# The last two product units of a stage taken chunk by chunk, with up to four output units of a feed-forward pass held back

## The chip, the cores and the metric

The kernel runs on one core of one Trainium2 chip. The metric is the device time of one execution in microseconds (us); the figure for a kernel is the median of its runs. TensorE (PE) multiplies matrices, VectorE (DVE), ScalarE (ACT) and GpSimd (POOL) work on tiles in on-chip memory, SyncE (SP) issues the DMA transfers that bring weights in.

## The reference

Two blocks work on x, 256 tokens of 1024 numbers. The first has two layers of `x = x + mixer(x); x = x + peer_ffn(x)`, where `peer_ffn` gathers from 16384 experts (128 units of 128). The second has two layers of

```python
x = x + 0.5 * m[2] * swiglu(modulate(x, norm_g[l, 0], m[0], m[1]), ffn1_wi[l], ffn1_wo[l])
if ctx_in:
    ctx = ctx + 0.5 * mc[2] * swiglu(modulate(ctx, norm_g[l, 0], mc[0], mc[1]), ffn1_wi[l], ffn1_wo[l])
h = modulate(x, norm_g[l, 1], m[3], m[4])
...
x = x + m[5] * y
...
x = x + 0.5 * m[8] * swiglu(modulate(x, norm_g[l, 2], m[6], m[7]), ffn2_wi[l], ffn2_wo[l])
```

with `swiglu(h, wi, wo)` = `(silu(a) * u) @ wo`, `a, u = split(h @ wi)`, 2816 wide (22 times 128). `modulate` is an RMS norm with a gain, a scale and a shift. `mc` and `ctx` are a second, 256 tokens long sequence, the context, which is used in the first of the two layers alone. At the end comes `rmsnorm(x, final_g)`.

## The kernel before, in words

**Data.** x is held transposed: 128 partitions, 8 chunks, 256 tokens. A weight unit is 128x1024 fp32. It is loaded (`raw`, L85), ACT rounds it to fp32r (`whi`, L93), and DVE or POOL makes the remainder (`wlo`, L97). The activations are split in the same way (`xnh` and `xnl`, `ch` and `cl`, `hh` and `hl`). Each product is three matmuls, hi by hi, hi by lo, lo by hi (`mm3`, L170 to L172), so that a unit takes 24 matmuls.

**Stages.** mix0, peer0, mix1, peer1, then ffn1_0, mixb0, ffn2_0 (layer 0 of the second block) and ffn1_1, mixb1, ffn2_1 (layer 1), then the final norm. All but the final norm end alike: `up` (L200) adds the last units into four PSUM banks with two chunks of 128x256 each (`acc`), and `residual` (L205) adds the eight chunks to x. The next stage begins with the norm of x: eight squares on ACT (`sq`, L225, two buffers), eight matmuls against ones (`nps`, L226), square root on ACT (`rstd`, L216), reciprocal on DVE (L217). Most stages take the norm's factor out of the product: `scaled` (L234) makes `xnh` and `xnl` from x alone, and the factor is applied to the products, so that the stage's first matmuls need x and not `rstd`. mixb0, mixb1 and the final norm need `rstd` first (`norm`, L260: `ny`, then `xnh` and `xnl`).

**A feed-forward pass** (`ffn`, L985). 22 rounds: two units `wi` (`ff`), SiLU and gate (`t`, `hh`, `hl`), one unit `wo` into `acc`. The output unit of a round is multiplied one round later (lag 1). A pass for x has a room (`Room`, L971) with its own stream of `wi` units of three buffers (`F_RAW`, `F_BUFS`), of which the first six `wlo` are made by POOL (`LEAD_I`); the `wo` units go through the main stream, also three buffers. The pass over the context `xc` works inside mixb0, in a room without a stream, and its matmuls stand among those of mixb0's projections.

**Order.** The order of each engine's instructions is found when the program is built, by a scheduler that takes the program's order as the priority and plays the engines through in time. A buffer that is used again adds a wait for its last reader. On-chip memory is handed out by rooms, so that a larger room takes addresses that another tile could have had.

Of the kernel before, what the change touches and what calls it, by code (L numbers as in the profile page):

```python
# [9 lines left out]
F32 = mybir.dt.float32  # L10
F32R = mybir.dt.float32r
I32 = mybir.dt.int32
U32 = mybir.dt.uint32
AF = mybir.ActivationFunctionType
OP = mybir.AluOpType
# [3 lines left out]
T = 256  # L19
NDC = 8  # L20
# [19 lines left out]
N_REC = 6  # L40
PAT_F = "v"
X_DMA = 4
F_RAW = 3
F_BUFS = 3
PAT_R = "v"
PAT_G = "v"
NF = 22

CAND = [(0, 1, 16, 0), (1, 2, 8, 16), (2, 4, 5, 24), (4, 8, 3, 34), (8, 16, 1, 46)]
NCAND = 54  # L50
# [50 lines left out]
class Net:  # L101
# [100 lines left out]
            s = slice(dc * 128, (dc + 1) * 128)  # L202
            self.mm3(acc[dc // 2][:, dc % 2], (w[0][:, s], w[1][:, s]), h, first and dc % 2 == 0, last)

    def residual(self, x, acc, gate=None):  # L205
        nc = self.nc
        for dc in range(NDC):
            if gate is None:
                nc.vector.tensor_tensor(out=x[:, dc], in0=acc[dc // 2][:, dc % 2], in1=x[:, dc], op=OP.add)
            else:  # L210
                nc.vector.scalar_tensor_tensor(out=x[:, dc], in0=acc[dc // 2][:, dc % 2], scalar=gate[:, dc:dc + 1],
                                               in1=x[:, dc], op0=OP.mult, op1=OP.add)
# [92 lines left out]
def hgrn_gmlp(n: Net):  # L305
    nc, d = n.nc, n.d
    n.rotation = ["mm", "ac", "mm", "ac", "mm", "ac", "ac"]
    n.stream.pattern = PAT_0
    with ExitStack() as st:
        p = st.enter_context(n.tc.tile_pool(name="m0", bufs=1, reuse_waits="tile"))  # L310
        w2 = st.enter_context(n.tc.tile_pool(name="m0w", bufs=2, reuse_waits="tile"))
        xn, rn = n.scaled(n.x, n.v("l0_norm_mix"), None, None, p)
# [152 lines left out]
        for h in range(4):  # L465
# [6 lines left out]
            nc.scalar.activation(out=q, in_=ps, func=AF.Square)  # L472
            squares.append([(q, 0, 128)])
        rs = n.head_rstd(p, sel, squares, 128)
        for h in range(4):
            y = w2.tile([128, T], F32, tag="y", name="y")
            nc.vector.scalar_tensor_tensor(out=y, in0=oo[:, h], scalar=n.v("hgrn_g")[:, h:h + 1], in1=rs[h],
                                           op0=OP.mult, op1=OP.mult)
            nc.vector.tensor_tensor(out=y, in0=y, in1=og[:, h], op=OP.mult)
            yh = w2.tile([128, T], F32R, tag="yh", name="yh")  # L480
            yl = w2.tile([128, T], F32R, tag="yl", name="yl")
            n.split(y, yh, yl)
            n.up(acc, n.unit(d["w0_out"][h]), (yh, yl), False, h == 3)
        n.residual(n.x, acc)

def peer(n: Net, layer, mod, mod_upto):
# [4 lines left out]
    with ExitStack() as st:  # L493
# [4 lines left out]
        xn = []  # L498
# [118 lines left out]
        with ExitStack() as sg:  # L617
            gp = sg.enter_context(n.tc.tile_pool(name="gg", bufs=1, reuse_waits="tile"))
            gg = gp.tile([128, 128 - NS, T], F32, name="gg")
            onehot = n.tc.tile_pool(name="oneh", bufs=OH, reuse_waits="tile")  # L620
            o2 = onehot.__enter__()
            for t0 in range(0, T, 4):
                a = o2.tile([128, 4, 128], F32, tag="oa", name="oa")
                b = o2.tile([128, 4, 128], F32, tag="ob", name="ob")
                g = n.bank("gps").rearrange("p (t e) -> p t e", t=4)


                by_act = t0 // 4 % N_ACT == 1
                for t in range(4):
                    at = lambda s: it[:, s, t0 + t:t0 + t + 1]  # L630
                    nc.vector.tensor_scalar(out=a[:, t], in0=n.iota, scalar1=at(0), scalar2=None, op0=OP.is_equal)
                    if by_act:
                        nc.scalar.activation(out=b[:, t], in_=n.iota, func=AF.Abs, scale=-1.0, bias=at(1))
                        nc.scalar.activation(out=b[:, t], in_=b[:, t], func=AF.Relu, scale=-2.0, bias=at(2))
                    else:
                        nc.vector.tensor_scalar(out=b[:, t], in0=n.iota, scalar1=at(1), scalar2=at(2),
                                                op0=OP.is_equal, op1=OP.mult)
                for t in range(4):
                    nc.tensor.matmul(g[:, t], a[:, t], b[:, t], start=t == 0, stop=True, skip_group_check=True)  # L639
                ge = g.rearrange("p t e -> p e t")  # L640
                nc.vector.tensor_tensor(out=ca[:, :, t0:t0 + 4], in0=ca[:, :, t0:t0 + 4], in1=ge[:, 0:NS], op=OP.mult)
                nc.scalar.copy(out=gg[:, :, t0:t0 + 4], in_=ge[:, NS:128])  # L642
            n.stream.pattern = PAT_G
            onehot.__exit__(None, None, None)
            g2 = sg.enter_context(n.tc.tile_pool(name="gg2", bufs=2, reuse_waits="tile"))

            def coef(i):
                return ca[:, i] if i < NS else gg[:, i - NS]

            acc = []  # L650

            def up(i):
                if not acc:
                    acc.extend(n.accs())
                w = n.unit(d[pre + "up"][i])
                c = coef(i)
                ch = g2.tile([128, T], F32R, tag="ch", name="ch")
                cl = g2.tile([128, T], F32R, tag="cl", name="cl")
                n.split(c, ch, cl)
                n.up(acc, w, (ch, cl), i == 0, i == 127)  # L660

            done = 0
            for i in range(NS, 128, 2):
                def sink(b):
                    nc.scalar.activation(out=b, in_=b, func=AF.Gelu_apprx_tanh)
                    c = gg[:, i - NS:i - NS + 2]
                    nc.vector.tensor_tensor(out=c, in0=c, in1=b, op=OP.mult)  # L667
                if i == NS + 2 * N_PARK:
                    while mod.next < mod_upto:
                        mod.step(n.main.raw_p)  # L670
                    mod.bank = None
                down_pair(i, sink, "ac" if i < NS + 2 * N_PARK else None)
                while i >= NS + 2 * N_PARK and done < i + 2 - N_LAG:
                    up(done)
                    done += 1
            while done < 128:
                up(done)
                done += 1
            n.residual(n.x, acc)

# [288 lines left out]
class Room:  # L971


    def __init__(self, n, st, tag, own=False):
        pool = lambda name, bufs: st.enter_context(n.tc.tile_pool(name=name + tag, bufs=bufs, reuse_waits="tile"))
        self.p = pool("f", 1)
        self.w2 = pool("g", 2 if own else 3)
        self.xn = pool("fx", 1) if own else None
        self.more = None if own else Stream(n, st, "f", F_RAW, F_BUFS)
        if not own:  # L980
            self.more.pattern = n.main.pattern = PAT_F
            self.more.lead, n.main.lead = LEAD_I, n.main.count + LEAD_O


def ffn(n: Net, x, mod, cond, which, wi, wo, gvec, tag, room=None):  # L985

    nc = n.nc
    with ExitStack() as st:
        room = room or Room(n, st, tag)
        p, w2 = room.p, room.w2  # L990
        gain = mod.gain(which + 1, cond, gvec)
        gate = mod.gate(which + 2, cond, 0.5)
        xn, r = n.scaled(x, gain, mod.m[:, which, cond], room.xn, p)
        acc = n.accs()
        late = None
        for f in range(NF + 1):
            if f < NF:
                t = []
                c = w2.tile([128, 2], F32, tag="c", name="c")
                for u in range(2):  # L1000
                    b = n.bank("ff")
                    w = (room.more or n).unit(wi[f, u])
                    n.proj_t(b[:, 0:T + 2], w, xn)
                    t.append(w2.tile([128, T], F32, tag=f"t{u}", name=f"t{u}"))
                    nc.vector.tensor_copy(out=c[:, u:u + 1], in_=b[:, T:T + 1])
                    nc.vector.tensor_tensor(out=t[u], in0=b[:, 0:T], in1=r, op=OP.mult)
                s = t[0]
                nc.scalar.activation(out=s, in_=s, func=AF.Silu, bias=c[:, 0:1])
                hh = w2.tile([128, T], F32R, tag="hh", name="hh")
                hl = w2.tile([128, T], F32R, tag="hl", name="hl")  # L1010
                if f < NF - 1:
                    nc.vector.scalar_tensor_tensor(out=s, in0=t[1], scalar=c[:, 1:2], in1=s, op0=OP.add, op1=OP.mult)
                    n.split(s, hh, hl)
                else:
                    for o in (hh, s):
                        nc.vector.scalar_tensor_tensor(out=o, in0=t[1], scalar=c[:, 1:2], in1=s, op0=OP.add, op1=OP.mult)
                    nc.vector.tensor_tensor(out=hl, in0=s, in1=hh.bitcast(F32), op=OP.subtract)  # L1017
                now = (f, n.main.unit(wo[f]), (hh, hl))
            if late is not None:
                n.up(acc, late[1], late[2], late[0] == 0, late[0] == NF - 1)  # L1020
            late = now
        n.residual(x, acc, gate)


def gla_decay(n, p, w2, zg, wa2, tag, smask):
# [613 lines left out]
```

## Time and profile before

| | us |
|---|---|
| runs | 3463.34, 13268.22, 3464.38 |
| median | 3464.38 |
| profiled execution | 3467.64 |
| its span in the trace | 3465.9 |
| PE busy | 3313.4 |
| DVE busy | 2193.9 |
| ACT busy | 1649.2 |
| POOL busy | 179.0 |

The run of 13268.22 stands apart from the two others. The profiled execution is 1.7 us longer than its span and 3.3 us longer than the median. Stages by the span's clock: mix0 ends at about 186, peer0 at 1114, mix1 at 1274, peer1 at 2206, ffn1_0 at 2408, mixb0 at 2813, ffn2_0 at 3023, ffn1_1 at 3217, mixb1 at 3250, ffn2_1 at 3451, and the final norm at the span's end.

In a timeline row the first number is the start, the second the time from there to the end of the group; in brackets stands how long the engine had been idle, and what ended that.

### The profile page before, as it was taken

What the parts mean: (1) busy time and instruction counts of PE and PEld (TensorE: products, weight loads), DVE (VectorE), ACT (ScalarE), POOL (GpSimd) and SP (SyncE); (2) the same over time, 40 slices, a digit from 0 to 9 for tenths busy, and PEclk for the clock granted to TensorE, in tenths of its full rate; (3) what the DMA queues carried; (4) which work ended last, traced back from release to release, by engine and by line L of the source; (5) the groups of instructions that cost most, each with busy time, mean ns of one, the idle gap of its engine ahead of it and who ended that gap; (6) DMA issues with size and microseconds to landing.
All of it is one profiled execution on the core that took longest, in us unless ns stands there. A gap on an engine that the chain in (4) does not pass through costs nothing.

```text
span 3465.9 us, 65621 instructions
## 1 busy us (share of the span) xinstructions
PE 3313.4 (96%) x26734; PEld 3150.2 (91%) x26734; DVE 2193.9 (63%) x4589; ACT 1649.2 (48%) x2609; POOL 179.0 (5%) x93
## 2 busy tenths in 40 slices
PE   7999998999999999998999999999999989999798
PEld 6789977999999779996899999999999779999698
DVE  6389487555556559759555555666766656666665
ACT  5445455444444344445445444544644444454443
POOL 2200000000000310000000000100000020100200
PEclk9999999999999999999999999999999999999899
DMA  6645544556555545545556555554444235454353
GB/s 227 230 159 182 178 156 161 183 183 207 183 183 170 199 157 166 177 158 182 195 183 231 183 183 183 182 183 143 158 165 147 86 123 187 165 183 156 132 187 105
DMA packets 165759, 597.79 MB, mean 172 GB/s; under 512 B 18512, under 2 KB 20176, under 8 KB 165072
## 3 DMA queue, kind: packets, MB, share of 16 engines
q1 hardware_dynamic: 165456, 593.59, 51.5%
q8 instruction: 210, 3.44, 0.4%
q14 instruction: 93, 0.76, 0.1%
HBM read 592.47 MB, written 1.05 MB: 171 GB/s over the span
## 4 chain that ended last, share of the span: by engine, by line
PE 83%; DVE 11%; DMA 2%; ACT 2%; issue 1%; POOL 0%; SPq 0%; ACTq 0%; DVEq 0%; POOLq 0%
PE acc L170 11%; PE acc L171 10%; PE acc L172 10%; PE dn L172 7%; PE dn L170 7%; PE dn L171 7%; PE ff L170 6%; PE ff L171 6%; PE ff L172 6%; DVE wlo L97 2%; PE mm L170 2%; PE mm L171 2%; PE mm L172 2%; PE mod L940 2%; DMA mraw<-w_mod 2%; PE gps L639 2%
## 5 line engine op out<-in xcount | busy, mean ns | idle before, releaser
L93 ACT CAST whi<-raw 128x1024 fp32r<-128x1024 f32 x973 | 1016.3, 1046 | 1398.9 <-PE acc L171 540.7
L97 DVE TENSOR_TENSOR wlo<-raw,whi 128x1024 fp32r<-128x1024 f32 x908 | 1111.6, 1225 | 841.8 <-ACT whi L93 841.3
L170 PE MATMUL dn<-xnh,whi 128*128 128x256 f32 x2048 | 582.3, 284 | 3.1 <-ACT gg L642 2.5
L172 PE MATMUL dn<-xnh,wlo 128*128 128x256 f32 x2048 | 581.8, 285 | 1.5 <-DVE wlo L97 1.5
L171 PE MATMUL dn<-xnl,whi 128*128 128x256 f32 x2048 | 581.5, 284 | 0.0
L171 PE MATMUL acc<-cl,whi 128*128 128x256 f32 x2048 | 561.6, 283 | 1.0 <-DVE cl L165 1.0
L172 PE MATMUL acc<-ch,wlo 128*128 128x256 f32 x2048 | 559.5, 283 | 0.0
L170 PE MATMUL acc<-ch,whi 128*128 128x256 f32 x2048 | 512.2, 283 | 0.2 <-DVE gg L667 0.2
L170 PE MATMUL ff<-xnh,whi 128*128 128x258 f32 x1760 | 504.6, 287 | 7.5 <-ACT rstd L216 4.0
L171 PE MATMUL ff<-xnl,whi 128*128 128x258 f32 x1760 | 502.8, 286 | 4.2 <-DVE xnl L247 4.2
L172 PE MATMUL ff<-xnh,wlo 128*128 128x258 f32 x1760 | 499.2, 284 | 3.5 <-POOL wlo L97 2.2
L170 PEld LDWEIGHTS dn<-xnh,whi 128*128 128x128 f32 x2048 | 395.0, 193 | 3.7 <-ACT gg L642 2.7
L172 PEld LDWEIGHTS dn<-xnh,wlo 128*128 128x128 f32 x2048 | 394.4, 193 | 2.2 <-DVE wlo L97 2.2
L171 PEld LDWEIGHTS dn<-xnl,whi 128*128 128x128 f32 x2048 | 395.0, 193 | 0.0
L171 PEld LDWEIGHTS acc<-cl,whi 128*128 128x128 f32 x2048 | 393.2, 192 | 1.5 <-DVE cl L165 1.5
L172 PEld LDWEIGHTS acc<-ch,wlo 128*128 128x128 f32 x2048 | 392.1, 192 | 0.0
L170 PEld LDWEIGHTS acc<-ch,whi 128*128 128x128 f32 x2048 | 363.7, 192 | 0.4 <-DVE gg L667 0.4
L170 PEld LDWEIGHTS ff<-xnh,whi 128*128 128x128 f32 x1760 | 334.8, 190 | 12.2 <-ACT rstd L216 5.2
L171 PEld LDWEIGHTS ff<-xnl,whi 128*128 128x128 f32 x1760 | 337.0, 192 | 6.3 <-DVE xnl L247 5.6
L172 PEld LDWEIGHTS ff<-xnh,wlo 128*128 128x128 f32 x1760 | 335.1, 191 | 4.9 <-POOL wlo L97 2.7
L97 POOL TENSOR_TENSOR wlo<-raw,whi 128x1024 fp32r<-128x1024 f32 (+1 forms) x65 | 157.7, 2433 | 2614.0 <-ACT whi L93 1968.6
L171 PE MATMUL acc<-hl,whi 128*128 128x256 f32 x880 | 246.9, 282 | 3.0 <-DVE hl L1017 3.0
(446 smaller groups left out, 5389.5 us busy)
## 6 DMA issues: line engine op xcount, KB each, us to landing
raw<-l_down SPq DMA_DIRECT2D x256, 512.0 KB, 3.4
raw<-l_up SPq DMA_DIRECT2D x256, 512.0 KB, 3.3
mraw<-w_mod SPq DMA_DIRECT2D x144, 512.0 KB, 4.4
raw<-f1i SPq DMA_DIRECT2D x132, 512.0 KB, 3.4
raw<-f2i SPq DMA_DIRECT2D x88, 512.0 KB, 3.9
raw<-f1o SPq DMA_DIRECT2D x66, 512.0 KB, 3.3
raw<-w_t SPq DMA_DIRECT2D x46, 512.0 KB, 3.6
raw<-f2o SPq DMA_DIRECT2D x44, 512.0 KB, 4.1
```

The lines of the kernel that those rows point to most:

```text
L93: nc.scalar.copy(hi[:, 0:k], raw[:, 0:k])
L97: eng.tensor_tensor(out=low[:, 0:k], in0=raw[:, 0:k], in1=hi.bitcast(F32)[:, 0:k], op=OP.subtract)
L170: mm(out, w[0], x[0], start=first, stop=False, skip_group_check=True)
L171: mm(out, w[0], x[1], start=False, stop=False, skip_group_check=True)
L172: mm(out, w[1], x[0], start=False, stop=last, skip_group_check=True)
L639: nc.tensor.matmul(g[:, t], a[:, t], b[:, t], start=t == 0, stop=True, skip_group_check=True)
L940: nc.tensor.matmul(ps[32 * j:32 * j + 32], n.cond[:, k], raw[:, j * T:(j + 1) * T], start=k == 0, stop=k == NDC - 1, tile_position=(0, 32 ...
```

## The change

`up_last` takes the products of the last two units by chunk: for each chunk of 128 columns three matmuls of either unit, then that chunk's residual. It takes the place of `up` and `residual` at the end of mix0 (heads 2 and 3), of both peers (units 126 and 127) and of the feed-forward passes. In a pass over x the output units 18 to 21 wait until the last `ff` unit is through: then units 18 and 19 come as before, and 20 and 21 chunk by chunk. For that the room has four buffers of the stream and of the tiles `t`, `hh`, `hl` where it had three, and unit 21's `wo` goes through the room's stream. The context's pass keeps lag 1, and its last unit is taken by chunk. The mixers mix1, mixb0 and mixb1 keep their code.

```diff
-F_RAW = 3
-F_BUFS = 3
+F_RAW = 4
+F_BUFS = 4
...
+N_LAST = 2
+F_LAST = 3
...
-    def residual(self, x, acc, gate=None):
+    def up_last(self, acc, units, x, gate=None):
+
+        for dc in range(NDC):
+            s = slice(dc * 128, (dc + 1) * 128)
+            for i, (w, h) in enumerate(units):
+                self.mm3(acc[dc // 2][:, dc % 2], (w[0][:, s], w[1][:, s]), h, False, i == len(units) - 1)
+            self.residual(x, acc, gate, (dc,))
+
+    def residual(self, x, acc, gate=None, chunks=range(NDC)):
         nc = self.nc
-        for dc in range(NDC):
+        for dc in chunks:
...
-            n.up(acc, n.unit(d["w0_out"][h]), (yh, yl), False, h == 3)
-        n.residual(n.x, acc)
+            last.append((n.unit(d["w0_out"][h]), (yh, yl)))
+            if h < 2:
+                n.up(acc, *last.pop(), False, False)
+        n.up_last(acc, last, n.x)
...
-                n.up(acc, w, (ch, cl), i == 0, i == 127)
+                if i < 128 - N_LAST:
+                    n.up(acc, w, (ch, cl), i == 0, False)
+                else:
+                    last.append((w, (ch, cl)))
...
-            n.residual(n.x, acc)
+            n.up_last(acc, last, n.x)
...
-        self.w2 = pool("g", 2 if own else 3)
+        self.w2 = pool("g", 2 if own else F_LAST + 1)
...
-                now = (f, n.main.unit(wo[f]), (hh, hl))
-            if late is not None:
-                n.up(acc, late[1], late[2], late[0] == 0, late[0] == NF - 1)
-            late = now
-        n.residual(x, acc, gate)
...
+            late.append((f, (more if more and f == NF - 1 else n.main).unit(wo[f]), (hh, hl)))
+            while len(late) > 1 and (f < NF - F_LAST or more is None):
+                i, w, h = late.pop(0)
+                n.up(acc, w, h, i == 0, False)
+        while len(late) > (N_LAST if more else 1):
+            i, w, h = late.pop(0)
+            n.up(acc, w, h, False, False)
+        n.up_last(acc, [u[1:] for u in late], x, gate)
```

How the order of the instructions moves is shown at three places. The first is PE at the end of ffn1_0, where the norm for mixb0 follows (`acc` are the last products, `nps` the norm's sums, `mm` mixb0's projections, `ff` the context's pass). Before:

```order
L170 MATMUL acc_25177<-hh,whi 128x256
L171 MATMUL acc_25177<-hl,whi 128x256
L172 MATMUL acc_25177<-hh,wlo 128x256
L226 MATMUL nps<-sq,ones 128x256 x4
L170 MATMUL ff<-xnh,whi 128x258
L171 MATMUL ff<-xnl,whi 128x258
L172 MATMUL ff<-xnh,wlo 128x258
```

After:

```order
L172 MATMUL acc_25177<-hh,whi 128x256
L173 MATMUL acc_25177<-hl,whi 128x256
L174 MATMUL acc_25177<-hh,wlo 128x256
L236 MATMUL nps<-sq,ones 128x256 x8
L172 MATMUL mm<-xnh,whi 128x256 x2
L173 MATMUL mm<-xnl,whi 128x256
L174 MATMUL mm<-xnh,wlo 128x256
```

Before, the context's `ff` stood between the norm's sums and the first `mm`; now all eight sums come first and the `mm`, which need the finished norm, come right behind them.

The second is SP's queue where the context is loaded (`xc`). Before, among the weights of peer1 (`l_down`, `l_up`):

```order
L85 DMA raw<-l_down 128x1024 [waits DMAHW3_49,DVE_49]
L85 DMA raw<-f1i 128x1024 [waits DVE_49]
L85 DMA raw<-f1i 128x1024 x2
L1083 DMA xc<-ctx_t 128x2048
L85 DMA raw<-l_up 128x1024 [waits DMAHW4_49,DVE_49]
```

After, behind mixb0's constants and after the weights of ffn1_0, with a wait for PE:

```order
L133 DMA c_gla<-c_gla 128x256 [waits DMAHW5_49]
L133 DMA c_axial<-c_axial 128x512 [waits DMAHW6_49]
L133 DMA w_a_27528<-w_a 128x512 [waits DMAHW7_49]
L1102 DMA xc<-ctx_t 128x2048 [waits DMAHW0_49,PE_49]
L87 DMA raw<-w_t 128x1024 [waits DMAHW1_49,DVE_49]
```

The load moved from peer1 to the end of ffn1_0; the PE instruction that it waits for is the last `ff` matmul of ffn1_0, four output units before the end of the pass.

The third is DVE at the end of peer1 (`x<-acc` is the residual, `xnl` the split of what ffn1_0 reads). Before:

```order
L165 TENSOR_TENSOR cl<-gg,ch 128x256 x2
L242 TENSOR_TENSOR xnl<-mod_83,xnh 128x8x2
L247 SCALAR_TENSOR_TENSOR xnl<-xc,mod_83,xnh 128x256 x3
L209 TENSOR_TENSOR x<-acc_18883,x 128x256 x2
L247 SCALAR_TENSOR_TENSOR xnl<-xc,mod_83,xnh 128x256 x2
L209 TENSOR_TENSOR x<-acc_18884,x 128x256 x2
L247 SCALAR_TENSOR_TENSOR xnl<-xc,mod_83,xnh 128x256
L209 TENSOR_TENSOR x<-acc_18885,x 128x256 x2
```

After:

```order
L167 TENSOR_TENSOR cl<-gg,ch 128x256 x2
L252 TENSOR_TENSOR xnl<-mod_83,xnh 128x8x2
L219 TENSOR_TENSOR x<-acc_18883,x 128x256
L219 TENSOR_TENSOR x<-acc_18884,x 128x256
L219 TENSOR_TENSOR x<-acc_18885,x 128x256
L219 TENSOR_TENSOR x<-acc_18886,x 128x256
L257 SCALAR_TENSOR_TENSOR xnl<-x,mod_83,xnh 128x256
L219 TENSOR_TENSOR x<-acc_18883,x 128x256
```

The residuals came in pairs, one bank after the other, with the context's `xnl` between; now the first chunk of each of the four banks comes, then the second of each, and the context's `xnl` are gone from here.

## Rows read from the trace of the kernel before

**Rows 1.** The page: busy time by engine, and the chain that ended last.

```profile
PE 3313.4 (96%) x26734; PEld 3150.2 (91%) x26734; DVE 2193.9 (63%) x4589; ACT 1649.2 (48%) x2609; POOL 179.0 (5%) x93
...
PE 83%; DVE 11%; DMA 2%; ACT 2%; issue 1%; POOL 0%; SPq 0%; ACTq 0%; DVEq 0%; POOLq 0%
```

**Rows 2.** The waits of PE: who waited for whom, us in total, times, longest.

```profile
PE nps L226 <- ACT sq L225: 20.2, 8, 6.9
```

**Rows 3.** Windows: stretch, length, busy us (instructions) per engine, granted clock, DMA share, GB/s.

```profile
2206.00:2212.00 6.00, 3.30 (x13) 1.77 (x11) 6.00 (x16) 6.00 (x13) 0.00 (x0) 0.78 0.54 203
2212.00:2216.00 4.00, 4.00 (x18) 4.00 (x19) 4.00 (x5) 3.46 (x8) 0.00 (x0) 0.50 0.77 246
...
3010.00:3016.00 6.00, 6.00 (x53) 5.99 (x51) 3.43 (x6) 3.66 (x6) 2.54 (x2) 1.00 0.28 89
3016.00:3019.00 3.00, 0.19 (x2) 0.00 (x0) 2.97 (x2) 0.84 (x1) 3.00 (x3) 0.88 0.47 164
3019.00:3025.00 6.00, 5.76 (x24) 5.49 (x25) 6.00 (x10) 2.82 (x6) 2.42 (x1) 0.50 0.11 29
...
1116.00:1122.00 6.00, 6.00 (x30) 4.20 (x30) 6.00 (x15) 4.97 (x11) 2.67 (x1) 0.63 0.30 76
```

**Rows 4.** Timeline of the last stage: end of ffn2_1 and the final norm.

```profile
3449.98 3.23 DVE L211 SCALAR_TENSOR_TENSOR x<-acc,mod,x 128x256 f32<-128x256 f32 x8 [1.85 <-PE acc L172]
...
3451.56 4.64 PE L226 MATMUL nps<-sq,ones 128*128 128x256 f32 x16
...
3457.27 1.75 DVE L217 RECIPROCAL rstd<-rstd 128x256 f32<-128x256 f32 x1 [4.06 <-ACT rstd L216]
3459.05 2.07 DVE L1434 SCALAR_TENSOR_TENSOR y<-x,vec,rstd 128x256 f32<-128x256 f32 x5
```

**Rows 5.** Timeline, PE at the end of ffn1_0: the three times it stood.

```profile
2410.62 0.39 PE L170 MATMUL ff<-xnh,whi 128*128 128x258 f32 x1 [0.95 <-DVE x L211]
2419.89 0.39 PE L170 MATMUL ff<-xnh,whi 128*128 128x258 f32 x1 [0.95 <-ACT rstd L216]
2424.05 0.36 PE L170 MATMUL ff<-xnh,whi 128*128 128x258 f32 x1 [1.03 <-DVE t L1006]
```

**Rows 6.** The DMA issues between 1870 and 1890 us: the load of the context.

```profile
xc<-ctx_t SPq DMA_DIRECT2D x1, 1024.0 KB, 9.3
```

**Rows 7.** Timeline of DVE and POOL at the end of ffn2_0.

```profile
3013.52 0.49 DVE L1016 SCALAR_TENSOR_TENSOR hh<-t,c,t 128x256 fp32r<-128x256 f32 x1
3014.04 2.67 DVE L1016 SCALAR_TENSOR_TENSOR t<-t,c,t 128x256 f32<-128x256 f32 x1
...
3014.03 7.39 POOL L97 TENSOR_TENSOR wlo<-raw,whi 128x1024 fp32r<-128x1024 f32 x3 [3.46 <-DVE hh L1016]
```

**Rows 8.** Timeline at the end of peer1, DVE and PE.

```profile
2206.24 0.28 PE L172 MATMUL acc<-ch,wlo 128*128 128x256 f32 x1
2206.36 0.87 DVE L247 SCALAR_TENSOR_TENSOR xnl<-xc,mod,xnh 128x256 fp32r<-128x256 f32 x2
...
2208.96 0.90 PE L226 MATMUL nps<-sq,ones 128*128 128x256 f32 x2 [2.44 <-ACT sq L225]
...
2209.26 0.75 DVE L209 TENSOR_TENSOR x<-acc,x 128x256 f32<-128x256 f32 x2
```

**Rows 9.** Timelines of PE, POOL and DVE at the end of peer0.

```profile
1114.66 2.08 PE L226 MATMUL nps<-sq,ones 128*128 128x256 f32 x4 [2.94 <-ACT sq L225]
...
1116.38 2.67 POOL L97 TENSOR_TENSOR wlo<-raw,whi 128x1024 fp32r<-128x1024 f32 x1 [4.71 <-ACT whi L93]
...
1116.74 0.74 DVE L209 TENSOR_TENSOR x<-acc,x 128x256 f32<-128x256 f32 x2
1117.41 1.93 DVE L247 SCALAR_TENSOR_TENSOR xnl<-x,vec,xnh 128x256 fp32r<-128x256 f32 x1
```

**Rows 10.** Timeline, PE at the end of mix0: the norm's first sums.

```profile
190.86 1.62 PE L226 MATMUL nps<-sq,ones 128*128 128x256 f32 x3 [2.18 <-DVE mod L950]
```

**Rows 11.** Timeline, PE at the end of ffn2_0: the first product of unit 21 with `hl`.

```profile
3019.24 0.58 PE L171 MATMUL acc<-hl,whi 128*128 128x256 f32 x1 [3.05 <-DVE hl L1017]
```

More of the change, by code (lines that the diff above doesn't have):

```diff
@@ L474, in hgrn_gmlp @@
         rs = n.head_rstd(p, sel, squares, 128)
+        last = []
         for h in range(4):
@@ L648, in coef @@
                 return ca[:, i] if i < NS else gg[:, i - NS]
-            acc = []
+            acc, last = [], []
             def up(i):
@@ L994, in ffn @@
         acc = n.accs()
[L995 to L1017, printed above, removed]
-                now = (f, n.main.unit(wo[f]), (hh, hl))
-            if late is not None:
-                n.up(acc, late[1], late[2], late[0] == 0, late[0] == NF - 1)
-            late = now
@@ L1022, in ffn @@
-        n.residual(x, acc, gate)
+        late, more = [], room.more
+        for f in range(NF):
+            t = []
+            c = w2.tile([128, 2], F32, tag="c", name="c")
+            for u in range(2):
+                b = n.bank("ff")
+                w = (room.more or n).unit(wi[f, u])
+                n.proj_t(b[:, 0:T + 2], w, xn)
+                t.append(w2.tile([128, T], F32, tag=f"t{u}", name=f"t{u}"))
+                nc.vector.tensor_copy(out=c[:, u:u + 1], in_=b[:, T:T + 1])
+                nc.vector.tensor_tensor(out=t[u], in0=b[:, 0:T], in1=r, op=OP.mult)
+            s = t[0]
+            nc.scalar.activation(out=s, in_=s, func=AF.Silu, bias=c[:, 0:1])
+            hh = w2.tile([128, T], F32R, tag="hh", name="hh")
+            hl = w2.tile([128, T], F32R, tag="hl", name="hl")
+            if f < NF - 1:
+                nc.vector.scalar_tensor_tensor(out=s, in0=t[1], scalar=c[:, 1:2], in1=s, op0=OP.add, op1=OP.mult)
+                n.split(s, hh, hl)
+            else:
+                for o in (hh, s):
+                    nc.vector.scalar_tensor_tensor(out=o, in0=t[1], scalar=c[:, 1:2], in1=s, op0=OP.add, op1=OP.mult)
+                nc.vector.tensor_tensor(out=hl, in0=s, in1=hh.bitcast(F32), op=OP.subtract)
+            late.append((f, (more if more and f == NF - 1 else n.main).unit(wo[f]), (hh, hl)))
+            while len(late) > 1 and (f < NF - F_LAST or more is None):
+                i, w, h = late.pop(0)
+                n.up(acc, w, h, i == 0, False)
```

## The prediction

> **What bounds the kernel now.** I read the page first. PE is busy for 3313.4 of 3465.9 us and is 83% of the chain of waits [rows 1]; the change takes no matmul away and adds none, so all that it can move is the 152 us in which PE stands, and the stretches in which its clock is low. The list of waits says which stands belong to a stage's end: the norm's sums wait for squares of x for 20.2 us, in eight places [rows 2]. The windows show what a stand costs behind itself: 53 matmuls fill 6 us at a clock of 1.00, which is 0.113 us each; PE then stands for nearly 3 us, and after it 24 matmuls take 5.76 us at 0.50, its 1.2 GHz level, which is 0.24 each [rows 3]. Behind the ends of peer1 and peer0 the same is seen, 18 matmuls in 4 us at 0.50 and 30 in 6 us at 0.63 [rows 3]. The timelines of each stage's end, read last, show who is late there. Below, E is the end of a stage's last product.
>
> **The change, end by end.** The new order of products takes nothing from PE inside a stage: a unit's 24 matmuls are 2.7 us in either order, and two units give 6 matmuls or 0.68 us a chunk, more than the 0.40 us of a residual (3.23 us for eight [rows 4]). So seven residuals are done by E and the eighth half a microsecond behind it, where before up to six came behind E. What that is worth hangs on what the next stage waits for.
>
> - *ffn2_1 to the final norm:* 0. The residuals end at 3453.21, but the eight sums behind E run until 3456.20, since ACT has two buffers for the squares and PE gives one free only behind the last product [rows 4]. The change leaves all eight sums behind E. The cover of the residual is this pacing, and it stays. ffn1_1 to mixb1 is built alike: I take -0.5, between -1 and 0.
> - *mix0 to peer0:* the sums at 190.86 come behind the modulation work, which ends 2.18 us of idle [rows 10], not behind x. -0.5, between -2.2 (that stand gone) and +1 (the next unit's cast is later, since two units are held to the end).
> - *peer0 to mix1:* PE stands 2.94 us [rows 9], and the 30 matmuls behind it, 3.4 us at full clock, take 6.0 [rows 3]: 5.5 us in all. DVE has the next stage's angles to work off beside the residuals, and the low clock comes with any long stand; I take -2, between -5.5 and +2.
> - *peer1 to ffn1_0:* PE stands 2.44 us for the squares [rows 8], and 18 matmuls behind it lose 2.0 us by the clock [rows 3]: 4.4 us. Two residuals come only at 2209.26, 2.9 us behind E (2206.36), because the context's `xnl`, 0.43 us each, stand between [rows 8]; these eight leave this place, as do the eight `xnh` on ACT. What comes in their place: the first `wlo` of ffn1_0, which POOL made during peer1, now wait for its last split, and four of them of 2.46 us each (7.39 us for three [rows 7]) fall on E. -2, between -4.4 and +4.
> - *ffn2_0 to ffn1_1:* unit 21's `hl` is late and PE stands 3.05 us for it [rows 11], because one `t` took 2.67 us where its twin `hh` took 0.49, beside three `wlo` on POOL [rows 7]; with the slow clock behind it (24 x 0.127 = 3.0 us [rows 3]) that is 6.1 us. Afterwards units 18 and 19, 48 matmuls or 5.4 us, stand between the last `ff` and unit 20, and POOL's `wlo` wait for a product of the last units. So this stand goes. What is late next is the first `wlo` of ffn1_1: it begins about E and takes 2.46, so that PE has the first two products of a chunk and not the third, and a stand of 2 to 3 us with its slow clock returns behind E. -1.5, between -6.1 and +4.
> - *ffn1_0 to mixb0:* here the change takes cover away. Before, the context's `ff` filled PE while x was normalised: it stood 0.95, 0.95 and 1.03 us, 2.9 in all [rows 5]. Those `ff` need the context, whose load now waits for the last `ff` of ffn1_0, behind eight constants in SP's queue; everything behind it on that queue waits too, but the first mixb0 weights stand ahead. From there to E are four units, 96 matmuls or 10.8 us, and the load takes 9.3 [rows 6]: it lands near E, but its splits stand behind x's norm on ACT and DVE. What PE then does behind its eight sums is seen in the final stage: from 3456.20 nothing until the first normalised chunk is begun at 3459.05 [rows 4], 2.85 us, and a split of two operations of some 0.43 behind that, 3.7 in all against 2.9. The slow clock follows: 3.0 us as behind ffn2_0's stand [rows 3]. Then each chunk needs a normalised x and two splits on DVE, 1.3 us, for about nine matmuls, 1.0 us: 8 x 0.3 is 2.4 us, of which the slow clock hides half. 0.8 + 3.0 + 1.2 = +5. The lower end is 0, if the clock stays up; the upper +12, if the context lands late and PE stands for four chunks more.
> - *Inside mixb0* the context's matmuls stand in other places among the projections. Their number is the same; I take 0, between -5 and +5, the size of the stands just named.
> - *Lag and buffers* inside a pass: 0. PE is full there, 53 matmuls in 6 us [rows 3]; a fourth buffer has nothing to hide.
>
> Sum: 0 - 0.5 - 0.5 - 2 - 2 - 1.5 + 5 + 0 = -1.5 us. The profiled execution was 3467.64, 3.3 us above the median of 3464.38; it would be 3466.1, and the median 3462.9, which I round to 3463.
>
> **The rivals.**
>
> *A, all of it comes back.* If x was the last thing that each next stage waited for, and the context costs nothing, peer0 gives 5.5, peer1 4.4 and ffn2_0 6.1: 16.0 us, 3448. For it: in two of these three places PE's stand ends with the squares of x [rows 8, 9]. Against it: casts, `wlo` and the norm are only microseconds behind. 0.17.
>
> *B, slower: the lost cover at ffn1_0's end.* The +12 above, with 3 us given back by the ends of peer0, peer1 and ffn2_0 together: +9, 3473. It decides from the point where that end loses more than the 6.5 us that I give the others. For it: the final stage shows the same chain without cover [rows 4], and the load's issue moved to E. Against it: SP's wait ends 10.8 us ahead of E. 0.22.
>
> *C, POOL's `wlo` hold the splits.* Beside POOL's `wlo` of 1116.38 two residuals took 0.74 us together, as elsewhere, but the `xnl` behind them took 1.93 [rows 9], and a `t` 2.67 [rows 7]. So an operation of DVE with both inputs in on-chip memory lasts until POOL is through, and one that reads PSUM does not. After the change four `wlo` stand at the ends of peer1 and ffn2_0, 9.8 us; each lets one `xnl` through, and the eight are ready only some 11 us behind E. Both ends then give 0 in place of -2 and -1.5: +2, 3466. 0.13.
> The Trainium skill (SBUF — State Buffer, section "SBUF: two separate sides") has this as a rule: GpSimd and a VectorE instruction with two inputs in SBUF share one pair of ports, which the first to start holds for its whole instruction. By that rule, which speaks against this change at those two ends, the time is this rival's; the rows just named agree with it.
>
> *D, it does not do what it says.* The residual was hidden everywhere by the two buffers of squares, as at the very end [rows 4], and the context's cover is made up by other `mm`: no change, 3464. Against it: two residuals 2.9 us behind E in peer1 [rows 8]. 0.13.
>
> **The numbers.** My forecast has 0.35, A 0.17, B 0.22, C 0.13, D 0.13. The forecast, C and D lie between 3460 and 3468. Taken singly the bounds reach from -24 to +28, but they would not all fall to one side; the range goes most of the way to A and just past B, 3450 to 3474. All cases are far inside 2% (69 us), which is about what a measurement of this kernel can tell from no change: faster 0.01, the same 0.97, slower 0.02.
>
> **What would show it.** In the changed profile: residuals in the order of banks 0, 1, 2, 3, 0, 1, 2, 3, the last one within 0.6 us of E; no wait of PE for `hl` at ffn2_0's end; at ffn1_0's end a stand of 3 us or more between the sums and the first `mm`, and a clock near 0.5 behind it; `xnl` of 2 us and more beside POOL at the ends of peer1 and ffn2_0. I am wrong if the clock stays at 1.00 behind ffn1_0, if the context lands long after E, or if mixb0's recurrence, which I did not follow, gains or loses more than 5 us by the new places of the context's matmuls.

## The result, and the profile after

The kernel after took 3489.1 us, the median of 6 runs (3482.3 to 3494.2); the kernel before took 3464.7 on the same chip. The ratio is 1.0072, with a 95% interval of 1.0059 to 1.0086: 24.4 us slower, well inside the 2% called no change and outside the predicted 3450 to 3474. The profiled execution took 3494.24 us, 5 above its median.

The page's row of PE, which answers to [rows 1]: PE is busy 18.8 us longer with the same 26734 matmuls, and the span grew by 26.6.

```profile
PE 3332.2 (95%) x26734; PEld 3164.7 (91%) x26734; DVE 2198.9 (63%) x4589; ACT 1647.2 (47%) x2608; POOL 178.9 (5%) x93
```

So less than a third, 7.9 us, is new idle time. By the clock's records of the two traces 11.0 us more are matmuls at the low clock, and the other 7.8 us are matmuls that stand further apart at full speed. The waits of PE after (us in total, times, longest), against [rows 2]:

```profile
PE mod L956 <- DMA mraw<-w_mod: 28.5, 30, 3.0
PE nps L236 <- ACT sq L235: 15.9, 9, 6.8
PE hrb L306 <- DVE hr L227: 9.6, 5, 3.0
...
PE mm L172 <- ACT xnh L285: 4.0, 1, 4.0
PE acc L173 <- DVE cl L167: 3.5, 2, 1.7
...
PE ff L172 <- ACT whi L95: 2.3, 3, 1.5
```

The wait for the squares fell by 4.3 us, and the 3.0 us for `hl` [rows 11] are gone: the chunk order does what it says. New or longer are a wait for `xnh` (ffn1_0's end), for `cl` (1.7 us each at the ends of peer0 and peer1, where it was 0.5 each), for casts (ffn2_0's end) and those in the second mix. These places, one by one.

**Second mix (mix1).** Timelines of SP and PE after: start, length, [idle before <-releaser].

```profile
1153.89 0.33 SPq L951 DMA_DIRECT2D mraw<-w_mod  x1
1156.22 7.88 SPq L87 DMA_DIRECT2D raw<-w_tok  x4
1172.63 0.33 SPq L951 DMA_DIRECT2D mraw<-w_mod  x1
...
1176.32 0.64 PE L956 MATMUL mod<-mraw,cond 128*32 128x256 f32 x8 [2.89 <-DMA mraw<-w_mod]
```

The same place before:

```profile
1157.07 1.08 SPq L935 DMA_DIRECT2D mraw<-w_mod  x2
1159.80 8.48 SPq L85 DMA_DIRECT2D raw<-w_tok  x4
...
1179.72 0.64 PE L940 MATMUL mod<-mraw,cond 128*32 128x256 f32 x8 [0.68 <-DMA mraw<-w_mod]
```

No line of the mix's code changed. But with peer0's new end the program's order behind it was drawn up anew, and now one modulation load, not two, stands ahead of the four `w_tok` loads in SP's queue. The next goes out at 1172.63, and PE stands for it. SP itself waited 8.5 us there, for a modulation step of PE (waits of SP between 1140 and 1200 us, after):

```profile
SPq L951 <- PE mod L956: 18.6, 5, 8.5
```

The waits for `hrb` grew as well, from 3.3 to 5.0 us.

Ahead of it, peer0's end itself gained nothing: from matmul 8400 to 8850 of the program both traces take the same time within 0.1 us. Before, PE stood there for `cl` and then 2.94 us for squares [rows 9]:

```profile
1109.06 0.39 PE L171 MATMUL acc<-cl,whi 128*128 128x256 f32 x1 [0.48 <-DVE cl L165]
```

Now it stands three times, 4.5 us in all, the first time for a `cl` that takes 2.43 us beside a split on POOL:

```profile
1105.71 0.38 PE L173 MATMUL acc<-cl,whi 128*128 128x256 f32 x1 [1.73 <-DVE cl L167]
1112.67 0.70 PE L236 MATMUL nps<-sq,ones 128*128 128x256 f32 x2 [0.94 <-ACT sq L235]
1117.19 0.38 PE L173 MATMUL mm<-xnl,whi 128*128 128x256 f32 x1 [1.80 <-DVE xnl L257]
```

**End of peer1.** Timelines of POOL, DVE and PE after:

```profile
2210.70 2.36 POOL L99 TENSOR_TENSOR wlo<-raw,whi 128x1024 fp32r<-128x1024 f32 x1 [943.92 <-ACT whi L95]
2213.42 9.74 POOL L99 TENSOR_TENSOR wlo<-raw,whi 128x1024 fp32r<-128x1024 f32 x4 [0.36 <-DVE cl L167]
...
2210.91 2.43 DVE L167 TENSOR_TENSOR cl<-gg,ch 128x256 fp32r<-128x256 f32 x1 [1.63 <-ACT ch L166]
2213.61 2.20 DVE L252 TENSOR_TENSOR xnl<-mod,xnh 128x16 fp32r<-128x16 f32 x1 [0.27 <-ACT xnh L251]
...
2213.40 0.39 PE L173 MATMUL acc<-cl,whi 128*128 128x256 f32 x1 [1.73 <-DVE cl L167]
2216.20 0.58 PE L172 MATMUL acc<-ch,whi 128*128 128x256 f32 x1 [1.59 <-DVE x L219]
2224.55 0.39 PE L172 MATMUL ff<-xnh,whi 128*128 128x258 f32 x1 [1.65 <-DVE x L219]
```

Before, POOL had one split five microseconds ahead of the end, and the next far behind it:

```profile
2201.13 2.40 POOL L97 TENSOR_TENSOR wlo<-raw,whi 128x1024 fp32r<-128x1024 f32 x1 [312.91 <-ACT whi L93]
2223.37 7.03 POOL L97 TENSOR_TENSOR wlo<-raw,whi 128x1024 fp32r<-128x1024 f32 x3 [19.84 <-ACT whi L93]
```

Now five in a row lie across the end (the last product starts at 2221.3). A `cl` of 0.42 us takes 2.43 beside them, an `xnl` of 16 columns 2.20, and PE stands inside its last units, for `cl` and, which the chunk order adds, for a residual. This is the holding of DVE by POOL that rival C took from [rows 7, 9]. The clock behind (windows: length, busy us (instructions) per engine, granted clock, DMA share, GB/s):

```profile
2217.00:2222.00 5.00, 5.00 (x25) 4.91 (x24) 5.00 (x6) 3.97 (x8) 5.00 (x3) 0.50 0.63 229
```

Half speed, 1.2 GHz, as behind the old stand [rows 3].

**End of ffn1_0.** Timelines of SP (the context's load) and PE after:

```profile
2423.32 0.37 SPq L1102 DMA_DIRECT2D xc<-ctx_t  x1
...
2423.47 3.54 PE L236 MATMUL nps<-sq,ones 128*128 128x256 f32 x12 [0.15 <-ACT sq L235]
2431.02 0.79 PE L172 MATMUL mm<-xnh,whi 128*128 128x256 f32 x2 [4.00 <-ACT xnh L285]
```

One stand of 4.00 us where there were 2.9 in three [rows 5], and 0.50 of the clock from 2431 to 2437.

**End of ffn2_0.** Timelines of PE, ACT, POOL and DVE after:

```profile
3042.62 0.39 PE L172 MATMUL ff<-xnh,whi 128*128 128x258 f32 x1 [1.46 <-ACT whi L95]
...
3031.57 1.05 ACT L95 CAST whi<-raw 128x1024 fp32r<-128x1024 f32 x1 [2.55 <-PE acc L173]
...
3041.54 3.87 ACT L95 CAST whi<-raw 128x1024 fp32r<-128x1024 f32 x4
...
3042.70 12.42 POOL L99 TENSOR_TENSOR wlo<-raw,whi 128x1024 fp32r<-128x1024 f32 x5 [7.59 <-ACT whi L95]
...
3045.86 4.67 DVE L257 SCALAR_TENSOR_TENSOR xnl<-x,mod,xnh 128x256 fp32r<-128x256 f32 x2 [2.69 <-ACT xnh L256]
```

The casts of weights on ACT now wait for the held-back products (`acc`, at 3031.57), which by the edit keep their buffers until the end, at 3040. Five casts follow from there in one lump, and POOL's splits behind them. Before, three splits lay at 3014 [rows 7], and four casts were made from 3012.85 on:

```profile
3012.85 2.00 ACT L93 CAST whi<-raw 128x1024 fp32r<-128x1024 f32 x2 [1.71 <-PE ff L171]
...
3014.85 1.99 ACT L93 CAST whi<-raw 128x1024 fp32r<-128x1024 f32 x2
```

### The profile page after: what moved, and what is told of

Read it like the earlier page. It is cut to its first block, busy times and chain, and to the rows that moved or that the text cites. A ratio compares the mean times of both kernels' runs of the same rounds, so it can differ in the third digit from the quotient of the medians.

```text
span 3492.5 us, 65597 instructions
## 1 busy us (share of the span) xinstructions
PE 3332.2 (95%) x26734; PEld 3164.7 (91%) x26734; DVE 2198.9 (63%) x4589; ACT 1647.2 (47%) x2608; POOL 178.9 (5%) x93
```

## The experiments

Each ran beside the kernel before on its chip, in five rounds. The table gives four stretches of each trace, from the start of one matmul to the start of another, counted in program order (numbers in the head), as difference from the trace of before in us. A single trace also catches its own low-clock stretches: the kernels whose order in mix1 is that of before differ there by up to 4 us among themselves. The last columns are medians and ratios.

| kernel | mix1 (8950 to 9550) | peer1's end (16900 to 17500) | ffn1_0's end (18700 to 19922) | ffn2_0's end (22900 to 23700) | median us | ratio [95%] |
|---|---|---|---|---|---|---|
| after | +10.2 | +3.7 | +2.8 | +4.8 | 3489.1 | 1.0072 [1.0059, 1.0086] |
| e1 | +10.6 | +0.3 | 0.0 | +0.2 | 3464.1 | 1.0003 [0.9992, 1.0014] |
| e2 | +3.2 | +2.2 | +2.4 | +3.1 | 3479.1 | 1.0050 [1.0035, 1.0065] |
| e3 | 0.0 | +1.8 | +3.5 | +1.8 | 3475.9 | 1.0038 [1.0025, 1.0050] |
| e4 | +7.7 | +0.4 | -2.6 | +2.8 | 3473.9 | 1.0033 [1.0022, 1.0044] |
| e5 | +3.0 | +0.7 | +0.2 | +0.6 | 3469.3 | 1.0011 [1.0000, 1.0021] |
| e7 | +4.1 | +1.6 | +2.5 | +0.2 | 3469.2 | 1.0014 [1.0003, 1.0024] |
| e8 | 0.0 | -0.3 | -0.4 | +3.0 | 3465.5 | 1.0001 [0.9990, 1.0012] |
| e10 | 0.0 | +3.7 | +1.3 | +3.1 | 3480.1 | 1.0060 [1.0043, 1.0077] |
| e11 | 0.0 | -0.2 | +0.2 | +1.6 | 3469.6 | 1.0018 [1.0005, 1.0031] |

**e1: chunk order in the first mix and the peer passes alone.** The feed-forward function and the room are those of before.

```diff
-F_RAW = 4
-F_BUFS = 4
+F_RAW = 3
+F_BUFS = 3
...
-        self.w2 = pool("g", 2 if own else F_LAST + 1)
+        self.w2 = pool("g", 2 if own else 3)
```

> Chunk by chunk at the ends of mix0 and both peers only; the feed-forward passes as before. Theory 1 (the loss is what the earlier end of peer0 does to the order inside mix1, plus what the larger feed-forward room displaces): about +10 us, nearly all inside mix1 between its 9100th and 9500th matmul of the kernel, nothing behind ffn1_0; about 3475. Theory 2 (the loss is at the ends themselves, where a product now waits for a residual of its bank): also about +10, but spread over the three ends at which the code stands, mix1's inside as before.

No change in the whole time (+1 us, -3 to +5), though its trace has the stand in mix1. At peer1's end, where no splits were moved, the wait of 2.4 us for squares [rows 8] is down to 0.9, and PE stands for x and for `cl` in its place (waits of PE between 2200 and 2225 us):

```profile
PE ff L172 <- DVE x L219: 2.1, 1, 2.1
PE acc L173 <- DVE cl L167: 1.7, 1, 1.7
```

So the chunk order by itself gains nothing at that end.

**e2: the reverse**, the feed-forward function, lag and room of the change, the rest as before.

```diff
...
-        n.up_last(acc, last, n.x)
+        n.residual(n.x, acc)
...
```

> Lag, four buffers and chunk by chunk in the feed-forward passes only; mix0 and peers as before. Theory 1: mix1 as before; +3 to +5 at the end of ffn1_0, +4 at the end of peer1, some +5 by a wider spacing of the matmuls in the passes, +5 at the end of ffn2_0: about +14, 3479. Theory 2: +12, all of it at the ends of the passes, spacing and end of peer1 as before.

+17 us (12 to 22): most of the loss comes with the feed-forward passes.

**e3: the kernel before with the larger room alone.**

```diff
-F_RAW = 3
-F_BUFS = 3
+F_RAW = 4
+F_BUFS = 4
...
-        self.w2 = pool("g", 2 if own else 3)
+        self.w2 = pool("g", 2 if own else 4)
```

> The kernel before with the larger room alone: four buffers of the stream and of t, hh, hl; no lag, no chunk by chunk. Theory 1: the context's load moves to the end of ffn1_0 as in the change, and the matmuls in the passes are 0.0015 us further apart: +8 to +12, about 3474. Theory 2: no change, 3465.

+13 us (9 to 17), with the code of the products unchanged; the order that is drawn up from it moves some of them at the ends of the stages. The prediction gave the buffers nothing.

**e4: the change in the small room**, holding back one unit less.

```diff
-F_RAW = 4
-F_BUFS = 4
+F_RAW = 3
+F_BUFS = 3
...
-F_LAST = 3
+F_LAST = 2
```

> The whole change but with the room before (three buffers), so that only up to three units are held back; the context's load is in peer1 again. Theory 1: mix1's +10 stays; the end of ffn1_0 is as before or better and the spacing as before: about 3477. Theory 2: as the change, 3489.

+11 us (8 to 15). Room (e3) and order (e4) thus make up about half of the 24.4 each, if the two add up, which no run shows place by place: at ffn1_0's end e3 has +3.5, e4 -2.6 and the change +2.8.

What the room costs was taken apart by two kernels that leave the code of the products as before.

**e5: an unused tile of 32 bytes in the room.** It shifts the room's tiles; the order on every engine is that of before.

```diff
         self.p = pool("f", 1)
+        if not own:
+            self.p.tile([128, 8], F32, tag="shift", name="shift")
```

> The kernel before with one unused tile of 32 bytes in the feed-forward room, so that hh, hl and the room's weights start at addresses that are 32 modulo 64, as in the change, and not 0; every engine's order is the same. Theory 1 (the wider spacing of the matmuls in the passes comes from the start addresses): 0.117 us between output products becomes 0.120 and the mean of the ff ones 0.1198 becomes 0.1206, 1.5 us for each of four passes, +6. Theory 2 (it comes from the fourth buffer, by more traffic at once): nothing moves.

+4 us (0 to 7). Windows of 100 us inside the last pass, where PE never stands: before, after, and e5.

```profile
3320.00:3420.00 100.00, 100.00 (x840) 100.00 (x839) 62.45 (x103) 46.21 (x58) 0.00 (x0) 1.00 0.56 180
```

```profile
3345.00:3445.00 100.00, 100.00 (x834) 100.00 (x833) 61.76 (x105) 45.98 (x58) 0.00 (x0) 1.00 0.54 175
```

```profile
3325.00:3425.00 100.00, 100.00 (x834) 100.00 (x833) 62.14 (x104) 45.37 (x57) 0.00 (x0) 1.00 0.54 182
```

At a clock of 1.00 and with PE full, 840 matmuls go through before, 834 after and in e5. The mean from start to start, worked out from the trace, went from 0.118 to 0.120 us for the products into `acc` and from 0.120 to 0.1205 for those into `ff`. A shift of 32 bytes does the same to the spacing as the change.

**e7: an unused tile of 16 KB in the room of before**, which the context's load has to wait for as it does in the change.

```diff
         self.p = pool("f", 1)
+        if not own:
+            self.p.tile([128, 4096], F32, tag="shift", name="shift")
```

> The kernel before with an unused tile of 16 KB in the feed-forward room: three buffers, start addresses at 0 modulo 64 as before, but the context's load waits for the end of ffn1_0 as in the change. Theory 1 (what the larger room displaces costs, not the buffers in it): +5 to +10, at the end of ffn1_0 and, by POOL's wlo, at the ends of peer1 and ffn2_0. Theory 2 (the fourth buffers cost): within 3 us of before.

+5 us (1 to 8). POOL's splits move onto peer1's end as in the change, and that end costs 1.6 us more. This timeline of POOL has them across the end at about 2204:

```profile
2201.24 8.02 POOL L97 TENSOR_TENSOR wlo<-raw,whi 128x1024 fp32r<-128x1024 f32 x3 [0.36 <-DVE cl L165]
```

Another 2.5 us lie at ffn1_0's end, where PE, which had stood 0.95 us for x [rows 5], waits for squares (between 2400 and 2425 us):

```profile
PE nps L226 <- ACT sq L225: 3.0, 2, 1.9
```

The change has no such wait there, so this part does not carry over to it. Together e5 and e7 make 9 of e3's 13 us; the other 4 lie within the intervals and are not taken apart.

**e8: the lag alone**, in the small room, no chunk order.

```diff
...
-        while len(late) > (N_LAST if more else 1):
+        while late:
             i, w, h = late.pop(0)
-            n.up(acc, w, h, False, False)
-        n.up_last(acc, [u[1:] for u in late], x, gate)
+            n.up(acc, w, h, False, not late)
+        n.residual(x, acc, gate)
```

> mix0 and peers as before, the room as before, and in the passes over x only the lag: units 19 to 21 wait until the last ff is through and come whole, then the residuals, as before. If the lag makes the loss of the small-room kernel (+12, of which the mixers' and peers' part is +2): +8 to +10. If the chunks make it: within 3 us.

+0.3 us (-3 to +4) in all, but ffn2_0's end loses 3.0. Its waits of PE there:

```profile
PE ff L173 <- DVE xnl L257: 3.5, 2, 1.9
PE ff L172 <- ACT whi L95: 1.1, 3, 0.4
```

The wait for `hl` is gone here as well, and is replaced by splits and casts: the lag, not the chunk order, turns one stand into the other.

**e10: the change with peer0's end as before.**

```diff
-                if i < 128 - N_LAST:
-                    n.up(acc, w, (ch, cl), i == 0, False)
+                if layer == 0 or i < 128 - N_LAST:
+                    n.up(acc, w, (ch, cl), i == 0, i == 127)
...
```

> The change, but peer0 ends as before (whole units, then the residuals). Theory 1 (peer0's earlier end lets mix1's modulation steps run out early and stand before a late load): mix1 is as before and the time falls by 7 to 10, to about 3480. Theory 2 (mix1's loss in the traces is the slow clock's chance): as the change within 3 us, 3488.

The stretch of mix1 is back to before's. Windows of 1160 to 1230 us, e10, after, and before:

```profile
1160.00:1230.00 70.00, 62.43 (x455) 43.39 (x455) 32.48 (x70) 21.90 (x43) 16.67 (x7) 1.00 0.56 195
```

```profile
1160.00:1230.00 70.00, 58.10 (x397) 38.36 (x396) 30.77 (x61) 17.66 (x34) 14.41 (x7) 0.94 0.47 166
```

```profile
1160.00:1230.00 70.00, 62.39 (x455) 43.35 (x454) 32.31 (x70) 22.33 (x45) 16.67 (x7) 1.00 0.56 197
```

In all seven kernels with the changed end of peer0, PE is busy 57.6 to 59.2 us there (e13 to e17: 16 us earlier, where this work lies in them); in the twelve others 62.3 to 62.6. So 4 us of idle time in mix1 come from the new end of peer0: shown. The clock varies in both groups (0.92 to 1.00), so its share is not. And the whole time of e10 lies only 4 us under that of the change, with intervals that overlap.

**e11: only the last unit of a feed-forward pass by chunk, small room, the rest as before.**

```diff
-N_LAST = 2
-F_LAST = 3
+N_LAST = 1
+F_LAST = 0
...
```

> mix0, peers and room as before, lag 1; in the passes over x only the last unit goes chunk by chunk. If chunks at the ends of the passes cost by themselves (a product waits for its bank's residual): +3 to +6, seen as a wait of an output product for x. If they do not: within 3 us of before; what the chunks save at ffn2_0's end is at most 3 us.

+6 us (2 to 11), of which the table shows 1.6. Where the rest goes stays open.

**e6 and e12: operands at multiples of 64 bytes**, in the kernel before and in the change.

```diff
-        self.vec = self.cp.tile([128, NVEC], F32, name="vec")
+        both = self.cp.tile([128, NVEC + 6], F32, name="vec")
+        self.vec, self.eps = both[:, 0:NVEC], both[:, NVEC + 2:NVEC + 3]
...
-                c = w2.tile([128, 2], F32, tag="c", name="c")
+                c = w2.tile([128, 16], F32, tag="c", name="c")[:, 0:2]
```

> The kernel before with start addresses at multiples of 64 bytes for most matmul operands (the 4-byte eps moves into the unused end of vec, c takes 64 bytes, the chunks of xnh and xnl lie 1088 bytes apart): 22714 of 25110 matmuls have both operands so, before 960. Theory 1: the peers' and mixers' matmuls, 0.120 us apart before, come to 0.117 or less: some 20000 x 0.003 = 60 us less, 3400. Theory 2: nothing moves beyond 3 us.

> The change with the start addresses of the aligned kernel (multiples of 64 bytes for most operands). The same spacing as there, 0.114 us between output products; what is left of the change's loss without addresses shows against the aligned kernel before (3452): +15 to +19, 3469. If the aligned addresses cover the loss: 3455.

e6 took 3452.5 (0.9962 [0.9949, 0.9975]), 12 us less and not 60: `acc<-hh` in the passes went to 0.114 us, but the peer passes stayed at 0.120. e12 took 3486.7 (1.0075 [1.0059, 1.0090]), no gain, `acc` at 0.1195. So it is not the multiple of 64. What fits both is the distance of the two start addresses, of the moving operand and of the weights, modulo 128: it is 64 for `acc<-hh` in e6 (0.114), and 0 in the peer passes of before and e6 (0.120), in the passes of after and e5 (0.120) and in e12 (0.1195); 96 in the passes of before (0.118).

**e9: the change with the 32 byte tile of e5**, so that this distance is 32 in the passes.

> The change with one unused tile of 32 bytes in the feed-forward room, which brings hh, hl and the room's weights to start addresses at 0 modulo 64; every engine's order is that of the change. If the start addresses add to the rest as a term of their own: 0.117 us between output products, 1.5 us less for each of four passes, the change less 5 to 6, about 3483. If they matter only where nothing else is late: as the change, 3489.

The spacing of `acc` fell to 0.117, and 100 us of the last pass hold 844 matmuls. The time, 3484.0, ratio 1.0072 [1.0057, 1.0088], doesn't tell it from the change: 5 us lower as a median, the same as a ratio.

**e13: before, with one 576 byte tile moved behind the main weight buffers**, which makes the distance 64 in the peer passes. **e14, e15: before and the change with distance 64 in all passes.**

```diff
+        self.cp2 = pool("const2", 1)
...
-        self.m = n.cp.tile([128, 9, 2, NDC], F32, name=f"mod{layer}")
+        self.m = (n.cp if layer else n.cp2).tile([128, 9, 2, NDC], F32, name=f"mod{layer}")
```

> The kernel before with one tile (the first layer's modulation, 576 bytes) placed behind the main weight stream in on-chip memory and not ahead of it; every engine's order is the same. The main stream's weights then lie 64 bytes modulo 128 from the operand that they are multiplied with in 15336 of 25110 matmuls (942 before), and 0 in 1811 (16205 before). Theory 3 (the spacing depends on the distance modulo 128 of the two operands of a matmul, widest at 0): the peers' 0.120 us comes to about 0.114, 12288 x 0.006 = 71 us there and some 10 in the mixers, 3385. Theory 1 (start addresses by themselves, multiples of 64): no start address changes its remainder by 64, so nothing moves, 3463.

> As the kernel with the main stream moved, and in the passes over x too: xnh and xnl with chunks 1152 bytes apart, 32 bytes ahead of hh and 64 ahead of the room's weights, so that 21352 matmuls have the distance 64; every engine's order is that of before. Theory 3: also 0.114 us between output products of the passes and about 0.115 in ff, 6336 x 0.004 = 25 us more, 3360. Theory 1: within 3 us of before.

> The change with its operands at the same distances (64 in 21320 matmuls); every engine's order is that of the change. Theory 3: the same spacing as in the kernel before it was done to, so that what is left between the two is the change's loss by order and room alone: 15 to 20 us above that kernel, 3378. If the change's loss were only addresses, both would be equal.

e13 took 3430.8 us (0.9911 [0.9889, 0.9932]). Windows inside the first peer pass, before and e13:

```profile
600.00:1000.00 400.00, 400.00 (x3336) 400.00 (x3335) 215.29 (x258) 184.86 (x254) 0.00 (x0) 1.00 0.57 188
```

```profile
600.00:1000.00 400.00, 400.00 (x3399) 400.00 (x3398) 218.93 (x261) 188.64 (x258) 0.00 (x0) 1.00 0.56 192
```

0.1199 us a matmul became 0.1177. By 2.2 ns the 12288 matmuls of the peer passes give 27 of the 31 us, less than half of theory 3's 71. e14 took 3429.4 (0.9899 [0.9879, 0.9919]): it beats both kernels, by 1.0% the one before. But of the 25 us that theory 3 put beyond e13 nothing came: with most `ff` matmuls at distance 64 too, those stand 0.120 us apart as before. e15 took 3449.6 (0.9957 [0.9941, 0.9972]). At equal spacing the change is still 20 us slower than the old order.

**e16, e17: e14 and e15 with operands at multiples of 64 bytes as well.**

> The kernel before, same order of instructions, with the addresses of e14 and the one-column epsilon tile put into the tail of the vector tile, so that every operand of the large matmuls (peer passes and feed-forward passes) starts at a multiple of 64 bytes; moving operand and weights stay 64 bytes apart modulo 128. Theory A (spacing of two matmuls follows the distance and the multiple of 64, as in the accumulating matmuls of e6, 0.114 us): the 0.1178 us of e14 become 0.114 in the peer passes and the feed-forward passes; about 22,000 matmuls by 3.7 ns is 81 us, so 3345 to 3375 us. Rival B (0.114 was a property of the feed-forward accumulation of e6 alone, or another limit stands near 0.1178): peers stay at 0.117 to 0.118, time 3410 to 3432 us.

> The change, same order of instructions as it, with the addresses of e16. Theory A (what is left of the change's loss is its order, in the second mix and at the ends of the passes, and not the spacing): 15 to 25 us above e16, that is 3360 to 3400 us. Rival B (the rest of the loss hangs on spacing too): within 7 us of e16. Rival C (faster matmuls uncover more waits for the weight splits and squares of the change): over 30 us above e16.

e16 took 3432.7 (0.9905 [0.9878, 0.9932]), the spacing stayed at 0.1178, so the 0.114 of e6 needs something else. e17 took 3450.2 (0.9951 [0.9933, 0.9969]), 17.5 us above e16. With e14 and e15 that makes 17 to 20 us for the order and the displaced loads, and 4 to 7 of the 24.4 for the spacing; the four intervals reach 5 to 9 us to either side, so this division is rough.

## Why the prediction was wrong

**The step that failed first: "Lag and buffers inside a pass: 0. PE is full there".** PE was full, but that excludes only a gain. The larger room alone costs 13 us (e3): it moves the tiles' addresses, which costs 4 us (e5; 4 to 7 by the pairs e14, e15 and e16, e17), and it moves loads, which costs 5 (e7), of which the wait at ffn1_0's end is not in the change; 4 of the 13 stay open. Since a full PE has no cover, each nanosecond of a matmul shows; I did not consider that one could depend on an address.

**peer1 to ffn1_0, -2, was +3.7.** The mechanism stood in the prediction: the first `wlo` of ffn1_0 "now wait for its last split, and four of them ... fall on E". Five fell there, and the bound of +4 was close. The sum weighed them by their own time, and not by what they hold: DVE's `cl` and `xnl`, on which the chunk order depends (rival C had the `xnl`). Nor was there a gain for them to eat up: without the moved splits this end is +0.3 and +0.4 (e1, e4), since PE stands for `cl` and for x where it had stood for the squares.

**ffn2_0 to ffn1_1, -1.5, was +4.8** in the profile (2.1 to 4.8 in the seven kernels with the whole end changed). The stand for `hl` went, as said. What I named as late next, POOL's first `wlo`, costs only 0.4 us, because casts come first: PE stands for them three times, 2.3 us, since the held-back products keep the buffers, and e8 shows the same.

**peer0 to mix1, -2, was +10.2** in the profile. The end itself gave nothing: its stands changed from 0.48 and 2.94 us to 1.73, 0.94 and 1.80, since `cl` and `xnl` came late where the squares had been. I did not look beyond it. The order behind it is drawn up anew, with a load behind four others in SP's queue, and mix1 has 4 us more of idle time, which goes when peer0's end is put back (e10). How much of it reaches the whole time is not settled: traces give some 7 us with the clock, the medians of e1 and e10 1 and 4.

**ffn1_0 to mixb0, +5, was +2.8**, with the stand (4.00 against the 3.7 worked out) and the low clock where they were put. The context's load left SP about 1 us behind the last product, and not 10.8 us ahead of it, but no stand of PE comes of that. Inside mixb0 (matmul 19600 to 22300) the trace is 3.5 us longer, nearly all of it low clock; the prediction had 0, between -5 and +5. mix0's end and the last stage gave next to nothing, as predicted.

**Two readings of the prediction** are off and change no term by more than 0.6 us. The last product of peer1 ends at 2206.52 (2206.24 and 0.28 in [rows 8]), and 2206.36 is the start of a row of DVE. And a window counts the matmuls that its edges cut: 53 in 6 us are about 0.119 us from start to start, not 0.113, so that four units are 11.4 us, not 10.8.

**The rivals.** B, slower, had the side but not the place: it put all at ffn1_0's end, which gave 3 of the 24. C's mechanism is there at both of its ends. It makes peer1's worse than its 0, because the chunks wait for the held operations; at ffn2_0's the casts come ahead of it. By the rule of the Trainium skill (SBUF — State Buffer, section "SBUF: two separate sides") the one that starts first keeps the shared ports for its whole instruction; the `cl` of 2.43 us beside a `wlo` of 2.36 agrees. A and D fall.

**Open:** why chunk order in the passes' last units costs some 10 us more in e4 than e1 and e8 have together (11 against 1 and 0.3), to which the 6 us of e11 may belong; how much of the 11 us of additional low clock in the profile of after is its own; and e9's ratio.

## What to carry to other kernels

An edit that only enlarges buffers can move the addresses behind them and the loads that wait for the room: run the buffers alone, before judging the idea they were made for. When an end of a stage gets shorter, follow the queues into the next stage, since an unchanged stage may come out in another order. In a stretch where PE is full, count matmuls in an equal window of both traces: this finds a loss that no list of waits shows.

## What the runs showed of the hardware

The spacing of these 128x256 matmuls at full clock changed with the addresses alone, in kernels with the same order on every engine; what fits is the distance between the starts of the two operands in a partition. At a distance of 0 modulo 128 bytes it was 0.1195 to 0.120 us; at 64 it was 0.118 in the peer passes (e13 to e17), at 96 in the passes of before 0.118, at 32 in e9 0.117, and at 64 in e6 0.114. e6 and e16 both have 64 and multiples of 64, but the moving operand starts at 0 modulo 128 in e6 and the weights do in e16; whether that makes the 0.114 was not tried. Two cases don't fit: the context's pass of the kernel before has 96 too, and 0.1195 us; and the `ff` matmuls, 128x258, have 0.120 at 64 in e14 and 0.119 at 0 in e6. So the distance is not the whole of it. The Trainium skill (TensorE: Matmul & The Clock Gate, section "Step-by-step: what each phase is for") says that the weight load and the moving operand have read ports of their own, so that the one takes no bandwidth from the other. The 3336 and 3399 matmuls in 400 us, with the same order and other addresses, speak against a full independence; by which mechanism was not shown.
